# Gathering the tokens of four small experts together, from a normalised copy

## The chip, the cores and the metric

The kernel runs on one core of a Trainium2 chip. The metric is the time of one execution on the device in microseconds (us); three runs of the kernel before took 1511.56 to 1518.7 us, median 1512.85. One further execution was profiled. The engines are TensorE (PE in the profile, its weight loads PEld), VectorE (DVE), ScalarE (ACT), GpSimd (POOL) and SyncE (SP), which here issues every DMA of the weights from its one queue.

## The reference

Two layers of a streaming encoder on 256 tokens of width 1024, all in float32. Layer 0 ends in a dense SwiGLU, layer 1 in a mixture of eight experts of which each token takes two. The change lies in the last part alone:

```python
def moe_swiglu(xn, w_router, w_gate, w_up, w_down):     # xn = rmsnorm(h, norm_ffn_g)
    xt = xn.reshape(-1, d)
    logits = (xt @ w_router).astype(jnp.float32)
    top_vals, top_idx = lax.top_k(logits, TOP_K)
    top_w = jax.nn.softmax(top_vals, axis=-1)
    combine = jnp.sum(one_hot(top_idx, N_EXPERTS) * top_w[..., None], axis=1)
    y = jnp.zeros_like(xt)
    for e in range(N_EXPERTS):
        y = y + combine[:, e:e + 1] * swiglu(xt, w_gate[e], w_up[e], w_down[e])
    return y
# then h = h + y and a final rmsnorm of h
```

Each expert has two weights of 1024 x 3584 and one of 3584 x 1024. All eight are read, 336 loads of 1 MB.

## The kernel before, in words

**Weights.** Class `Stream` reads the weights in chunks of 128 partitions x 2048 floats (`dma`, line 172). `do_split` turns a chunk into two fp32r tiles: `hi` by ScalarE (line 198, a rounded copy) and `lo` by VectorE (line 199, what the rounding left). PE then multiplies with both. All raw chunks, the `hi` and `lo` tiles and a few long-lived ones share one pool of 21 buffers of 8 KB a partition (`R`). When chunk c is split, the load of chunk c+7 is issued (`WIDE_LOAD = 7`); splits run ahead of PE by up to five chunks. A load waits on SP's queue until the buffer that it was given is free, and everything behind it in that queue waits too.

**Places.** After the router, the experts are put in places 0 to 7: place 0 is expert 0, places 1 to 4 are the four experts with the fewest tokens of the others (at most 64 each, "small"), places 5 to 7 the rest (up to 128, "large"). A branch that handles fuller experts is not taken with these inputs. `merged` writes the order by hand: 56 blocks (a block is 512 of an expert's 3584 hidden columns), first three of place 0, then a small and a large one in turn, at the end three of place 4. A block has a gate product, a value product and a down product, each over two chunks; the down product comes two blocks later.

**Gather and scatter.** The tokens of a place are gathered by a product with a one-hot matrix. `Place.gather` makes two such tiles on VectorE: `pg` (line 1134), scaled by the token's 1/rms, and `pb` (line 1138), unscaled. Then PE multiplies 128 x 128 pieces of `h` (from block 3 on of `hs`, a saved copy, line 1303) with `pg` (line 1149): 16 matmuls for a place, of 64 columns for a small and 128 for a large one. ScalarE and VectorE take the result out of PSUM eight pieces at a time (`evict_bank`, lines 278 and 280), since each piece has its own gain column, and leave `xg`. Two transposes of `pb` (line 1157) give the scatter matrix `sc`. When a place's last down product is done, `half` evicts it as `y` (lines 272, 273), and four products `sc` x `y` (`part`, lines 1178 to 1180) add it to `h`.

**Order.** Each engine works in the order in which the code was written, so what is written early waits in front of what follows. Small pieces of PE work are put in a list `later`; `blocks` takes one off at four places of each block (after the gate product, before the down product, before and after the value product). `prepare` of a place makes its one-hot tiles at once, three blocks ahead of the place's first block, and puts its gather products and the transposes in `later`. `done` puts one empty piece and the four `part`s there.

**At the stage's start** the router's sorting steps (lines 1029 to 1059) and the combine weights (1074 to 1079, 1021 to 1024) run on VectorE between the first splits.

Of the kernel before, what the change touches and what calls it, by code (L numbers as in the profile page):

```python
# [21 lines left out]
F32R = mybir.dt.float32r  # L22
# [50 lines left out]

WIDE_LOAD = 7

# [9 lines left out]
def trunk(tc, x, xt_in, mem, mt_in, wa, wb, wc, wl0, wk1, wl1, wff, wmoe, cc, tk, moec, ident_d, gfin, out):  # L85
    nc = tc.nc
    PE, ACT, DVE, POOL = nc.tensor, nc.scalar, nc.vector, nc.gpsimd
    with contextlib.ExitStack() as c:
# [15 lines left out]
        def M(shape, dt=F32, s="m"):  # L104
            return mp.tile(shape, dt, name=nm(s), tag="m")
# [978 lines left out]
        class Final:  # L1084


            def load(self):
                self.x, self.g = R([P, NT, D], s="fin"), R([P, D], s="gf")
                nc.sync.dma_start(out=self.g, in_=gfin)
                self.rms = Rms(h)  # L1090
# [14 lines left out]
            def all(self, part):  # L1105
# [5 lines left out]
                for t in range(NT):  # L1111
                    for n in range(2):
# [3 lines left out]
                        nc.sync.dma_start(out=out[t * P:(t + 1) * P, w], in_=x)  # L1116

        class Place:


            def __init__(self, run, i, small):
                self.run, self.i, self.small = run, i, small
                self.n = HALF if small else P

            def gather(self):

                i, n = self.i, self.n
                slot, r, src = self.run.slot, self.run.r, self.run.src

                def one_hot():  # L1130
                    self.pg = M([P, NT, n], s="pg")
                    self.back_ = M([P, NT, P], s="pb")
                    for t in range(NT):
                        DVE.tensor_scalar(self.pg[:, t, :], iota[:, 0:n], slot[:, t, i:i + 1], r[:, t:t + 1],
                                          op0=OP.is_equal, op1=OP.mult)
                    for t in range(NT):
                        q = P // n
                        DVE.tensor_scalar(self.back_[:, t, :].rearrange("p (q n) -> p q n", q=q),
                                          iota[:, 0:n].unsqueeze(1).to_broadcast([P, q, n]),
                                          slot[:, t, i:i + 1], None, op0=OP.is_equal)  # L1140
                    self.xg = R([P, KC, 2, n], F32R, s="xg")

                def block(k0):
                    m = 512 // n
                    ps = mm()
                    for j in range(m):
                        kk = slice((k0 + j) * P, (k0 + j + 1) * P)
                        for t in range(NT):
                            PE.matmul(ps[:, j * n:(j + 1) * n], src(t)[:, kk], self.pg[:, t, :],  # L1149
                                      start=t == 0, stop=t == NT - 1)  # L1150
                    evict_bank([(self.xg[:, k0 + j, 0], self.xg[:, k0 + j, 1], ps[:, j * n:(j + 1) * n],
                                 col(1, C_FFN + k0 + j)) for j in range(m)])

                def back():
                    ps = mm()
                    for t in range(NT):
                        PE.transpose(ps[:, tok(t)], self.back_[:, t, :], ident)
                    self.scat = M([P, S], F32R, s="sc")
                    ACT.activation(self.scat, ps[:, 0:S], AF.Copy)

                return [one_hot] + [lambda k=k: block(k) for k in range(0, KC, 512 // n)] + [back]
# [21 lines left out]
            def done(self):  # L1183
                later.append(lambda: None)
                for n in range(2):
                    for t in range(NT):
                        later.append(lambda t=t, n=n: self.part(t, n))

        class Block:
# [7 lines left out]
            def product(self, x, out, items, first, last):  # L1197

                if self.small:
                    ops = [(x[0][:, f].rearrange("p i s -> p (i s)"), it[i]) for i in range(2) for f, *it in items]  # L1200
                else:
                    ops = [(x[i][:, f], w) for f, wh, wl in items for i, w in ((0, wh), (0, wl), (1, wh))]
                for i, (a, w) in enumerate(ops):
                    PE.matmul(out, a, w, start=first and i == 0, stop=last and i == len(ops) - 1)  # L1204

            def up(self, out):
                for c in range(2):
                    items = []
                    for i, (wh, wl) in enumerate(self.st.many(2)):
                        items += [(4 * c + 2 * i + q, wh[:, q * 512:(q + 1) * 512], wl[:, q * 512:(q + 1) * 512])  # L1210
                                  for q in range(2)]
                    xg = self.place.xg
                    self.product((xg, None) if self.small else (xg[:, :, 0], xg[:, :, 1]), out, items, c == 0, c == 1)

# [46 lines left out]
            def parts(self):  # L1261
                n = self.place.n
                if self.small:
                    t = M([P, 4, 2, n], F32R, s="hl")
                    self.hl = t, None
                    hi, lo = t[:, :, 0], t[:, :, 1]
                else:
                    hi, lo = self.hl = [M([P, 4, n], F32R, s="hl") for _ in range(2)]
# [21 lines left out]
        class Run:  # L1290
# [4 lines left out]

            def src(self, t):
                return self.saved[0][:, t, :] if self.saved else h[t]
# [71 lines left out]
        def moe(st, routed, weights, sort, combine):  # L1369
# [19 lines left out]
            before = {}  # L1389
            at = {x: i for i, x in enumerate(order)}  # L1390

            def add(i, f):
                before.setdefault(i, []).append(f)
            add(LEAD, run.save)
            for p in range(1, NE):
                add(max(1, at[p, 0] - 3), places[p].prepare)
            run.blocks(st, [(places[p], j) for p, j in order],
                       {i: lambda fs=fs: [f() for f in fs] for i, fs in before.items()})

        def moe_rest(routed):  # L1400
# [8 lines left out]
            st.wide = True  # L1409
            for f in places[0].gather():  # L1410
                f()
            run.blocks(st, [(places[p], j) for p, j in order],
# [137 lines left out]
def _layout(a):  # L1550
# [43 lines left out]
    f["ident"] = np.eye(P, dtype=np.float32)  # L1594
    f["gfin"] = np.ascontiguousarray(np.broadcast_to(a["norm_final_g"][None], (P, D)))
    return f
# [26 lines left out]
```

## Time and profile before

| | |
|---|---|
| median of three runs | 1512.85 us (1511.56 to 1518.7) |
| profiled execution | 1510.55 us, of which span 1508.7 us |
| PE busy | 1469.5 us (97%) |
| DVE busy | 1293.9 us (86%) |
| ACT busy | 1043.2 us (69%) |
| DMA | 459.04 MB, mean 304 GB/s |
| granted TensorE clock | 0.989 of full speed |

The span is the time from the first to the last instruction of the program; 1.85 us of the execution lie around it. The experts' stage begins at about 595 us with the first gather and ends at 1493 us with the last product. Busy PE is not PE at its peak, since matmuls overlap and their ends are modelled; the chain of waits and the distances between matmuls say more. Many matmuls in plain float32 stand in the trace as two records each.

### The profile page before, as it was taken

To read this page: it belongs to the slowest core of one execution; us is meant where nothing else is said; L and a number is where in the kernel's file an instruction comes from. 1 tells how busy PE (TensorE), PEld (TensorE's weight loads), DVE (VectorE), ACT (ScalarE), POOL (GpSimd) and SP (SyncE) were. 2 spreads that over 40 slices of the span, in tenths; PEclk is the share of its full clock that TensorE was granted. 3 is DMA by queue.
4 is the path that set the end of the run, shared out by engine and by line. 5 is a ranking of instruction groups with operands and counts; after the bars stand their busy time and mean duration, and the time that the engine had idled before them with its cause. 6 is when DMAs were issued, how large, how long until landed. Compare 5 with 4: busy or idle time off the path is not lost.

```text
span 1508.7 us, 20807 instructions
## 1 busy us (share of the span) xinstructions
PE 1469.5 (97%) x7757; PEld 1270.9 (84%) x7757; DVE 1293.9 (86%) x1496; ACT 1043.2 (69%) x1224; POOL 7.9 (1%) x23
## 2 busy tenths in 40 slices
PE   8999999999999998999999999999999999999995
PEld 7998988888999897788887878888888888888884
DVE  7988777545698866889999999999999999999996
ACT  7547565434544554688887788887878887888884
POOL 0000000000000001000000000000000000000000
PEclk9999999999999998899999999999999999999998
DMA  9535464544542547399999999999999999999992
GB/s 363 236 112 195 156 247 159 210 178 156 178 178 116 195 168 307 124 376 401 421 381 421 360 403 413 416 386 411 366 397 414 411 392 386 390 403 415 421 421 86
DMA packets 65326, 459.04 MB, mean 304 GB/s; under 512 B 7232, under 2 KB 7744, under 8 KB 11840
## 3 DMA queue, kind: packets, MB, share of 16 engines
q1 hardware_dynamic: 65216, 457.62, 76.5%
q8 instruction: 63, 1.03, 0.3%
q14 instruction: 47, 0.39, 0.1%
HBM read 456.55 MB, written 1.05 MB: 303 GB/s over the span
## 4 chain that ended last, share of the span: by engine, by line
PE 90%; DVE 4%; issue 2%; ACT 2%; DMA 1%; POOL 0%; SPq 0%; DVEq 0%; ACTq 0%; POOLq 0%
PE mm L1204 31%; PE acc L1204 16%; PE mm L220 5%; PE mm L222 5%; PE mm L221 5%; PE mm L1227 3%; PE acc L221 3%; PE acc L222 3%; PE acc L220 3%; PE mm L463 3%; PE z L221 2%; PE z L222 2%; PE z L220 2%; DVE lo L199 2%; PE mm L1149 2%
## 5 line engine op out<-in xcount | busy, mean ns | idle before, releaser
L199 DVE TENSOR_TENSOR lo<-w,hi 128x2048 fp32r<-128x2048 f32 (+3 forms) x504 | 946.4, 1917 | 56.9 <-ACT hi L198 37.8
L198 ACT ACTIVATE hi<-w 128x2048 fp32r<-128x2048 f32 (+3 forms) x504 | 795.1, 1619 | 111.9 <-PE mm L1204 58.0
L1204 PE MATMUL mm<-hi,xg 128*128 128x512 f32 x1344 | 405.4, 393 | 1.6 <-ACT xg L278 1.2
L1204 PEld LDWEIGHTS mm<-hi,xg 128*128 128x128 f32 x1344 | 253.0, 189 | 53.7 <-ACT xg L278 1.4
L1204 PE MATMUL mm<-lo,xg 128*128 128x512 f32 x896 | 295.3, 391 | 0.0
L1204 PE MATMUL acc<-hi,hl 128*128 128x512 f32 x672 | 217.4, 398 | 0.0
L1204 PEld LDWEIGHTS mm<-lo,xg 128*128 128x128 f32 x896 | 168.8, 188 | 34.1
L1204 PE MATMUL acc<-lo,hl 128*128 128x512 f32 x448 | 157.7, 393 | 0.0
L1204 PEld LDWEIGHTS acc<-hi,hl 128*128 128x128 f32 x672 | 125.2, 189 | 24.4
L1204 PEld LDWEIGHTS acc<-lo,hl 128*128 128x128 f32 x448 | 84.8, 189 | 17.4
L220 PE MATMUL z<-hi,xt 128*128 128x320 f32 (+1 forms) x256 | 79.0, 308 | 7.0 <-ACT xt L338 7.0
L221 PE MATMUL z<-lo,xt 128*128 128x320 f32 (+1 forms) x256 | 77.9, 304 | 0.2 <-DVE lo L199 0.2
L222 PE MATMUL z<-hi,xt 128*128 128x320 f32 (+1 forms) x256 | 78.0, 304 | 0.0
L548 DVE SCALAR_TENSOR_TENSOR ca<-ca,cct 128x256 f32<-128x256 f32 x180 | 77.1, 482 | 0.2
L220 PE MATMUL mm<-hi,xt 128*128 128x512 f32 (+1 forms) x192 | 71.9, 375 | 0.0
L222 PE MATMUL mm<-hi,xt 128*128 128x512 f32 (+1 forms) x192 | 71.5, 372 | 0.0
L221 PE MATMUL mm<-lo,xt 128*128 128x512 f32 (+1 forms) x192 | 71.4, 372 | 0.0
L1227 PEld LDWEIGHTS mm<-twice,gu 128*128 128x128 f32 x448 | 58.3, 191 | 6.0 <-ACT gu L1217 2.1
L1227 PE MATMUL mm<-twice,gu 128*128 128x64 f32 x448 | 56.2, 268 | 2.0 <-ACT gu L1217 2.0
L220 PEld LDWEIGHTS z<-hi,xt 128*128 128x128 f32 x256 | 49.7, 194 | 7.2 <-ACT xt L338 7.0
L221 PEld LDWEIGHTS z<-lo,xt 128*128 128x128 f32 x256 | 49.6, 194 | 0.5 <-DVE lo L199 0.5
L222 PEld LDWEIGHTS z<-hi,xt 128*128 128x128 f32 x256 | 49.5, 193 | 0.0
(284 smaller groups left out, 1891.5 us busy)
## 6 DMA issues: line engine op xcount, KB each, us to landing
w<-in_wmoe_dram SPq DMA_DIRECT2D x336, 1024.0 KB, 8.0
w<-in_wl_dram SPq DMA_DIRECT2D x39, 1024.0 KB, 4.8
w<-in_wff_dram SPq DMA_DIRECT2D x33, 1024.0 KB, 4.8
w<-in_wb_dram SPq DMA_DIRECT2D x8, 960.0 KB, 8.9
w<-in_wa_dram SPq DMA_DIRECT2D x5, 1024.0 KB, 4.9
w<-in_wc_dram SPq DMA_DIRECT2D x8, 640.0 KB, 4.6
tk<-in_tk_dram SPq DMA_DIRECT2D x2, 1024.0 KB, 10.5
mt<-in_mem_t_dram SPq DMA_DIRECT2D x2, 1024.0 KB, 8.2
```

The source lines that it names most:

```text
L198: ACT.activation(hi[:, ws], r, AF.Copy)
L199: DVE.tensor_tensor(lo[:, ws], r, hi[:, ws].bitcast(F32), op=OP.subtract)
L220: PE.matmul(ps, ah, bh, start=start, stop=False)
L221: PE.matmul(ps, ah, bl, start=False, stop=False)
L222: PE.matmul(ps, al, bh, start=False, stop=stop)
L463: PE.matmul(self.kps[:, d, :], w[:, ks], self.mt[:, k, :], start=k == 0, stop=k == KC - 1)
L548: return lambda: DVE.scalar_tensor_tensor(dst, src[:, k:k + S], w, dst, op0=OP.mult, op1=OP.add)
L1149: PE.matmul(ps[:, j * n:(j + 1) * n], src(t)[:, kk], self.pg[:, t, :], start=t == 0, stop=t == NT - 1)
L1204: PE.matmul(out, a, w, start=first and i == 0, stop=last and i == len(ops) - 1)
L1227: PE.matmul(ps[:, f * n:(f + 1) * n], w, twice, start=True, stop=True)
```

## The change

The saved copy of the tokens is now normalised: `save` writes `hn` = h x 1/rms (ScalarE, two instructions) x gain (VectorE, two instructions; the gain comes by a new DMA of 512 KB, `gn`). It is made at block 1 instead of block 3. All four small places are gathered from it by one set of products with a 256-column one-hot `pgs` (`gather_small`): four pieces of PE work, each four matmuls and one eviction by ACT and one by DVE of 128 x 512. Large places 5 to 7 are gathered from `hn` with `pb` itself, so their `pg` is gone, and they too are evicted 512 columns at a time. Place 0 is gathered as before, but its `pb` is made after the sorting. A small place's `pb` and `sc` are made at its last block. `prepare` puts an empty piece in front, `done` two instead of one. `WIDE_LOAD` is 6 instead of 7.

```diff
-WIDE_LOAD = 7
+WIDE_LOAD = 6
...
-            def gather(self):
-                i, n = self.i, self.n
-                slot, r, src = self.run.slot, self.run.r, self.run.src
+            def gather_raw(self):
+                pg = M([P, NT, P], s="pg")
                 def one_hot():
-                    self.pg = M([P, NT, n], s="pg")
-                    self.back_ = M([P, NT, P], s="pb")
...
+                    self.hot(pg, self.run.r)
+                    self.xg = R([P, KC, 2, P], F32R, s="xg")
...
+                return [one_hot, lambda: block(0), lambda: block(4), self.spread, self.back]
+            def gather(self):
+                self.xg = R([P, KC, 2, P], F32R, s="xg")
+                def block(k0):
                     ps = mm()
+                    for j in range(4):
+                        kk = slice((k0 + j) * P, (k0 + j + 1) * P)
+                        for t in range(NT):
+                            PE.matmul(ps[:, j * P:(j + 1) * P], self.run.saved[0][:, t, kk], self.pb[:, t, :],
+                                      start=t == 0, stop=t == NT - 1)
+                    evict_hl(self.xg[:, k0:k0 + 4, 0], self.xg[:, k0:k0 + 4, 1],
+                             ps.rearrange("p (k s) -> p k s", k=4))
+                return [lambda: block(0), lambda: block(4)]
             def prepare(self):
-                first, *rest = self.gather()
-                first()
-                later.extend(rest)
+                self.spread()
+                later.append(lambda: None)
+                if not self.small:
+                    later.extend(self.gather())
+                later.append(self.back)
...
             def done(self):
-                later.append(lambda: None)
+                later.extend([lambda: None] * 2)
...
+            def load(self):
+                self.g = R([P, D], s="gn")
+                nc.sync.dma_start(out=self.g, in_=gfin[1])
             def save(self):
-                self.saved.append(R([P, NT, D], s="hs"))
-                for t in range(NT):
-                    ACT.activation(self.saved[0][:, t, :], h[t], AF.Copy)
+                hn = R([P, NT, D], s="hn")
+                self.saved.append(hn)
+                for t in range(NT):
+                    ACT.activation(hn[:, t, :], h[t], AF.Copy, scale=self.r[:, t:t + 1])
+                for t in range(NT):
+                    DVE.tensor_tensor(hn[:, t, :], hn[:, t, :], self.g, op=OP.mult)
+            def gather_small(self, places):
+                pg = M([P, NT, SMALL * HALF], s="pgs")
+                for q, p in enumerate(places):
+                    p.hot(pg[:, :, q * HALF:(q + 1) * HALF])
+                xs = [R([P, 4, SMALL, 2, HALF], F32R, s="xs") for _ in range(2)]
...
+                def block(k0):
+                    ps = mm()
+                    for j in range(2):
+                        kk = slice((k0 + j) * P, (k0 + j + 1) * P)
+                        for t in range(NT):
+                            PE.matmul(ps[:, j * 256:(j + 1) * 256], self.saved[0][:, t, kk], pg[:, t, :],
+                                      start=t == 0, stop=t == NT - 1)
+                    to = xs[k0 // 4][:, k0 % 4:k0 % 4 + 2]
+                    evict_hl(to[:, :, :, 0], to[:, :, :, 1], ps.rearrange("p (k q s) -> p k q s", k=2, q=SMALL))
+                return [lambda k=k: block(k) for k in range(0, KC, 2)]
...
-            first = places[0].gather()
-            later.append(first.pop())
-            later.append(combine)
-            for i, f in enumerate(first):
+            first = places[0].gather_raw()
+            for i, f in enumerate(first[:3]):
                 f()
                 if i == 0:
                     for _ in range(PRESPLIT):
                         st.do_split()
                     weights()
+                    run.load()
             sort()
+            first[3]()
+            later.extend([first[4], combine])
...
-            add(LEAD, run.save)
+            def start_small():
+                run.save()
+                later.append(lambda: None)
+                later.extend(run.gather_small(places[1:1 + SMALL]))
+            add(1, start_small)
             for p in range(1, NE):
-                add(max(1, at[p, 0] - 3), places[p].prepare)
+                add(max(2, at[p, 0] - 3) if p > SMALL else at[p, NJ - 1], places[p].prepare)
```

`hot` and `spread` write the one-hot tiles `pg`/`pgs` (line 1152 of the new kernel) and `pb` (line 1161). In the new kernel lines 1234, 1256, 1258 are the old 1204, 1227, 1229, and lines 1208 to 1210 the old 1178 to 1180.

First place, VectorE at block 1 of place 0, before: `lo` are splits, `a` is the gated product of block 0, `pg` and `pb` belong to place 1, the first small one, `xg` is its gathered input, `hl` the split of block 0's hidden values.

```order
L199 TENSOR_TENSOR lo_5845<-w_5694,hi_5844 128x2048
L199 TENSOR_TENSOR lo_5861<-w_5696,hi_5860 128x2048
L1247 TENSOR_TENSOR a_5825<-mm_5843,a_5825 128x512
L1134 TENSOR_SCALAR pg_5877<-mct,slotp,t_5611 128x64 x2
L1138 TENSOR_SCALAR pb_5878<-mct,slotp 128x128 x2
L199 TENSOR_TENSOR lo_5886<-w_5698,hi_5885 128x2048
L199 TENSOR_TENSOR lo_5914<-w_5700,hi_5913 128x2048
L280 SCALAR_TENSOR_TENSOR xg_5883<-mm_5933,cct,xg_5883 128x64 x8
L1271 TENSOR_TENSOR hl_5972<-mm_5966,hl_5971 128x512
```

The same place now:

```order
L199 TENSOR_TENSOR lo_5847<-w_5691,hi_5846 128x2048
L199 TENSOR_TENSOR lo_5863<-w_5693,hi_5862 128x2048
L1276 TENSOR_TENSOR a_5827<-mm_5845,a_5827 128x512
L1337 TENSOR_TENSOR hn_5879<-hn_5879,gn_5721 128x1024 x2
L1152 TENSOR_SCALAR pgs_5884<-mct,slotp 128x64 x8
L199 TENSOR_TENSOR lo_5897<-w_5695,hi_5896 128x2048
L199 TENSOR_TENSOR lo_5913<-w_5697,hi_5912 128x2048
L1301 TENSOR_TENSOR hl_5948<-mm_5942,hl_5947 128x512
L273 TENSOR_TENSOR xs_5893<-mm_5951,xs_5893 128x8x64
```

Where two one-hots of 64 columns and two of 128 stood between `a` and the next splits, two products of 128 x 1024 and eight one-hots of 64 columns stand now.

Second place, TensorE in the middle of the stage, before: the end of a large block's gate product, the gather of place 2 (`pg`, `hs`), then the transposes of a small block (`gu`) and a small block's down product (`acc`).

```order
L1204 MATMUL mm_7485<-lo_7423,xg_6845 128x512
L1204 MATMUL mm_7485<-hi_7422,xg_6845 128x512
L1149 MATMUL mm_7524<-pg_7478,hs_6142 128x64 x16
L1227 MATMUL mm_7557<-twice,gu_7469 128x64 x4
L1157 MATMUL mm_7563<-ident,pb_7479 128x128 x2
L1204 MATMUL acc_7568<-hi_7441,hl_7418 128x512
```

The same place now:

```order
L1234 MATMUL mm_7459<-lo_7400,xg_6838 128x512
L1234 MATMUL mm_7459<-hi_7399,xg_6838 128x512
L1256 MATMUL mm_7498<-twice,gu_7446 128x64 x4
L1234 MATMUL acc_7504<-hi_7418,hl_7395 128x512
```

The gather and the two transposes of place 2 are gone from here; the gather is in the four pieces at the start, the transposes are at place 2's last block.

Third place, TensorE where the output of place 1 is first read, before: `y` is the evicted down product, and it is read right behind a value product.

```order
L1204 MATMUL mm_7958<-hi_7900,xg_7484 128x512 x4
L1204 MATMUL mm_7958<-lo_7901,xg_7484 128x512 x4
L1178 MATMUL mm_7989<-y_7949,sc_5978 128x512
L1179 MATMUL mm_7989<-y_7949,sc_5978 128x512
L1227 MATMUL mm_7993<-twice,gu_7914 128x64 x4
L1204 MATMUL mm_8000<-hi_7921,xg_6845 128x512
```

The same place now (24 matmuls of the next gate product are cut to their first and last):

```order
L1234 MATMUL mm_7902<-lo_7845,xs_5894 128x512 x4
L1256 MATMUL mm_7933<-twice,gu_7858 128x64 x4
L1234 MATMUL mm_7940<-hi_7865,xg_6838 128x512
...
L1234 MATMUL mm_7940<-hi_7883,xg_6838 128x512
L1208 MATMUL mm_7979<-y_7893,sc_7625 128x512
L1209 MATMUL mm_7979<-y_7893,sc_7625 128x512
```

The first reading of `y` has moved behind the transposes and a whole gate product.

## Rows read from the trace of the kernel before

**Rows 1.** The page: busy times, and GB/s in 40 equal slices of the span.

```profile
PE 1469.5 (97%) x7757; PEld 1270.9 (84%) x7757; DVE 1293.9 (86%) x1496; ACT 1043.2 (69%) x1224; POOL 7.9 (1%) x23
...
GB/s 363 236 112 195 156 247 159 210 178 156 178 178 116 195 168 307 124 376 401 421 381 421 360 403 413 416 386 411 366 397 414 411 392 386 390 403 415 421 421 86
```

**Rows 2.** Stretches: us, busy PE, PEld, DVE, ACT, POOL, PEclk, DMA share, GB/s.

```profile
829.70:1051.10 221.40, 218.52 (x1065) 183.33 (x1065) 212.62 (x149) 180.49 (x148) 0.00 (x0) 1.00 0.99 399
1200.00:1300.00 100.00, 98.35 (x484) 82.43 (x482) 95.90 (x70) 81.66 (x69) 0.00 (x0) 1.00 0.95 381
```

**Rows 3.** Who waited for whom, 640 to 1508: us, times, longest.

```profile
ACT hi L198 <- PE mm L1204: 58.0, 57, 3.0
...
PE mm L1179 <- DVE y L273: 4.5, 5, 1.2
PE mm L1149 <- DVE pg L1134: 4.4, 3, 1.5
```

**Rows 4.** Waits of SP's own queue, 640 to 1508.

```profile
SPq L172 <- PE mm L1204: 360.3, 154, 5.1
SPq L172 <- PE acc L1204: 227.9, 84, 7.1
SPq L172 <- DVE lo L199: 63.1, 35, 5.9
```

**Rows 5.** Tile w (raw chunks), 640 to 1508: duration ns min/median/max.

```profile
L199 DVE TENSOR_TENSOR lo<-w,hi x324: 2280/2290/2307, 639.4 to 1484.9; 128x2048 fp32r<-128x2048 f32 x162
...
L172 SPq DMA_DIRECT2D w<-in_wmoe_dram x315: 327/333/788, 647.1 to 1465.0; - x158
...
DMA to landing us min/median/max: 4.7/8.1/14.2
```

**Rows 6.** Chain of waits before place 3's gather: start, us, what.

```profile
1049.54 1.17 issue
1050.71 0.33 DVE pg L1134
...
1051.08 3.79 PE mm L1149 x32
```

**Rows 7.** Chain of waits at the output of place 2.

```profile
1108.47 0.70 DVE y L273
...
1109.21 0.50 PE mm L1179
```

**Rows 8.** Groups by form: busy us, mean ns, idle before.

```profile
L1149 PE MATMUL mm<-pg,hs 128*128 128x128 f32 x96 | 11.7, 275 | 0.0
L1149 PE MATMUL mm<-pg,hs 128*128 128x64 f32 x96 | 11.4, 277 | 4.4 <-DVE pg L1134 4.4
...
L280 DVE SCALAR_TENSOR_TENSOR xg<-mm,cct,xg 128x128 fp32r<-128x128 f32 x32 | 8.6, 345 | 3.1 <-ACT xg L278 3.1
...
L280 DVE SCALAR_TENSOR_TENSOR xg<-mm,cct,xg 128x64 fp32r<-128x64 f32 x32 | 6.5, 276 | 5.2 <-ACT xg L278 5.2
```

**Rows 9.** Groups by form before 590: a float32 product of 256 columns.

```profile
L463 PE MATMUL mm<-mt,w 128*128 128x256 f32 x176 | 39.1, 381 | 0.0
```

**Rows 10.** Order of time at the stage's start: start us, us, instruction.

```profile
622.58 0.69 DVE L1247 TENSOR_TENSOR a<-mm,a 128x512 f32<-128x512 f32 x1
623.18 0.53 DVE L1134 TENSOR_SCALAR pg<-mct,slotp,t 128x64 f32<-128x64 f32 x2
623.63 0.48 DVE L1138 TENSOR_SCALAR pb<-mct,slotp 128x128 f32<-128x128 f32 x2
623.64 6.38 PE L1149 MATMUL mm<-pg,h 128*128 128x64 f32 x32 [3.14 <-DVE pg L1134]
...
630.94 0.78 PE L1204 MATMUL mm<-hi,xg 128*128 128x512 f32 x1
```

**Rows 11.** Stretches of TensorE: us, busy, PEclk, DMA share, GB/s.

```profile
623.00:624.00 1.00, 0.36 (x4) 1.00 0.52 74
624.00:634.60 10.60, 10.60 (x46) 0.52 0.23 94
634.60:640.00 5.40, 5.40 (x25) 1.00 0.61 206
```

More of the change, by code (lines that the diff above doesn't have):

```diff
@@ L1088, in load @@
                 self.x, self.g = R([P, NT, D], s="fin"), R([P, D], s="gf")
-                nc.sync.dma_start(out=self.g, in_=gfin)
+                nc.sync.dma_start(out=self.g, in_=gfin[0])
                 self.rms = Rms(h)
@@ L1116, in all, with part @@
                         nc.sync.dma_start(out=out[t * P:(t + 1) * P, w], in_=x)
+        def part(x, i):
+            return x[i] if type(x) is tuple else x[:, i]
         class Place:
@@ L1154, in back @@
-                def back():
-                    ps = mm()
[L1156 to L1161, printed above, removed]
-            def prepare(self):
-                first, *rest = self.gather()
-                first()
-                later.extend(rest)
+                    evict_bank([(self.xg[:, k0 + j, 0], self.xg[:, k0 + j, 1], ps[:, j * P:(j + 1) * P],
+                                 col(1, C_FFN + k0 + j)) for j in range(4)])
@@ new lines, in gather_raw, with hot @@
+                return [one_hot, lambda: block(0), lambda: block(4), self.spread, self.back]
+            def hot(self, out, r=None):
+                for t in range(NT):
+                    c = self.run.slot[:, t, self.i:self.i + 1]
+                    if r is None:
+                        DVE.tensor_scalar(out[:, t, :], iota[:, 0:self.n], c, None, op0=OP.is_equal)
+                    else:
+                        DVE.tensor_scalar(out[:, t, :], iota[:, 0:self.n], c, r[:, t:t + 1], op0=OP.is_equal, op1=OP.mult)
@@ new lines, in spread, with back @@
+            def spread(self):
+                self.pb = M([P, NT, P], s="pb")
+                for t in range(NT):
+                    q = P // self.n
+                    DVE.tensor_scalar(self.pb[:, t, :].rearrange("p (q n) -> p q n", q=q),
+                                      iota[:, 0:self.n].unsqueeze(1).to_broadcast([P, q, self.n]),
+                                      self.run.slot[:, t, self.i:self.i + 1], None, op0=OP.is_equal)
+            def back(self):
+                ps = mm()
+                for t in range(NT):
+                    PE.transpose(ps[:, tok(t)], self.pb[:, t, :], ident)
+                self.scat = M([P, S], F32R, s="sc")
+                ACT.activation(self.scat, ps[:, 0:S], AF.Copy)
@@ new lines, in gather @@
+            def gather(self):
+                self.xg = R([P, KC, 2, P], F32R, s="xg")
+                def block(k0):
+                    ps = mm()
+                    for j in range(4):
+                        kk = slice((k0 + j) * P, (k0 + j + 1) * P)
[5 more added lines that the diff above has]
+                return [lambda: block(0), lambda: block(4)]
@@ L1199, in product @@
                 if self.small:
-                    ops = [(x[0][:, f].rearrange("p i s -> p (i s)"), it[i]) for i in range(2) for f, *it in items]
+                    ops = [(x(f).rearrange("p i s -> p (i s)"), it[i]) for i in range(2) for f, *it in items]
                 else:
-                    ops = [(x[i][:, f], w) for f, wh, wl in items for i, w in ((0, wh), (0, wl), (1, wh))]
+                    ops = [(part(x(f), i), w) for f, wh, wl in items for i, w in ((0, wh), (0, wl), (1, wh))]
                 for i, (a, w) in enumerate(ops):
@@ L1211, in up @@
                                   for q in range(2)]
-                    xg = self.place.xg
-                    self.product((xg, None) if self.small else (xg[:, :, 0], xg[:, :, 1]), out, items, c == 0, c == 1)
+                    self.product(self.place.x(), out, items, c == 0, c == 1)
             def copy(self, ps):
@@ L1264, in parts @@
                     t = M([P, 4, 2, n], F32R, s="hl")
-                    self.hl = t, None
+                    self.hl = lambda f: t[:, f]
                     hi, lo = t[:, :, 0], t[:, :, 1]
                 else:
-                    hi, lo = self.hl = [M([P, 4, n], F32R, s="hl") for _ in range(2)]
+                    hi, lo = t = [M([P, 4, n], F32R, s="hl") for _ in range(2)]
+                    self.hl = lambda f: (t[0][:, f], t[1][:, f])
                 v = self.a.rearrange("p (f s) -> p f s", f=4)
@@ L1409, in moe_rest @@
             st.wide = True
-            for f in places[0].gather():
-                f()
+            places[0].prepare()
+            while later:
+                pe_later()
             run.blocks(st, [(places[p], j) for p, j in order],
@@ L1594, in _layout @@
     f["ident"] = np.eye(P, dtype=np.float32)
-    f["gfin"] = np.ascontiguousarray(np.broadcast_to(a["norm_final_g"][None], (P, D)))
+    f["gfin"] = np.stack([np.broadcast_to(g[None], (P, D)) for g in (a["norm_final_g"], a["norm_ffn_g"][1])])
     return f
```

23 lines of the change are left out of this document (8 added, 15 removed).

## The prediction

> **What bounds the kernel now.** I read the page's busy line first: PE is busy for 97% of the span [rows 1]. That alone proves little, so next come the stretches of the experts' stage. One period of the stage (a small and a large expert, 84 loads of 1 MB, 221.4 us, so 2.64 us a load) has PE at 218.52, DVE at 212.62 and the DMA engines at a share of 0.99 with 399 GB/s [rows 2]. The reader is to see three resources within 4% of each other. Which of them is waited for? The list of waits answers: ACT's splits wait for PE to free a buffer (58.0 us), and SP's queue waits for PE to free one too (360.3 and 227.9 us, against 63.1 for DVE) [rows 3, 4]; PE is never kept waiting by a split or a load there. So PE is the bound, and it loses time only where a small instruction of DVE comes late: 4.4 us for one-hot tiles in three waits, 4.5 us for `y` in five [rows 3]. The chain shows both: DVE comes out of its splits, makes `pg`, and PE starts [rows 6]; DVE makes the lower half of `y`, and PE starts [rows 7]. Last I read the order of time at the stage's start, where PE idles for 3.14 us and then runs for some 10 us at half clock [rows 10, 11].
>
> **The change, part by part.**
>
> *Gather of the small places.* Before, each takes 32 records of 64 columns. They cost 11.4 us for 96, 0.119 each, and the records of 128 columns cost the same (11.7 us for 96) [rows 8]: below 128 columns the number of records sets the price. A whole place takes 3.79 us on PE with nothing beside it [rows 6]. Places 2 to 4 lose theirs: 3 x 3.79 = -11.4 us. In their stead the common gather has 16 matmuls, again 32 records, of 256 columns. The nearest row for those is 39.1 us for 176, 0.222 each [rows 9]: 7.1 us for all four places, 1.8 us a piece. It stands at the start and is counted there. Bounds for a record: 0.119 (as at 64 columns) to 0.476 (four times that, if columns alone counted), 3.8 to 15.2 us in all; I take the row of the same width and type.
>
> The Trainium skill (TensorE: Matmul & The Clock Gate, Back-to-back issue gap) gives about 109 ns for a warm matmul of 256 columns. By that, as an estimate, the 32 records would take 3.5 us and the sum would come 3.6 us lower; this case's float32 row shows twice the page's figure, and I go by the row.
>
> *Waits for one-hots.* The three late `pg` tiles are those of places 2 to 4 (the first waits are gone with their gather): -4.4 us [rows 3]. A large place now needs only `pb`, made a piece earlier than it is read; a piece is at least 16 matmuls of a weight product, several us, and the lateness was at most 1.5 us [rows 3].
>
> *Output read a piece later.* What was late by up to 1.2 us now has the next gate product ahead of it: -4.2 us of the 4.5, since the last place's output stands at the end with nothing behind to cover it. Next late there would be the splits, which kept ahead of PE throughout.
>
> *DVE and ACT in the middle.* A period's DVE loses eight small evictions (6.5/32 x 8 = 1.6 us), turns eight larger ones (2.15 us, at 8.6/32) into two of 512 columns (about 1.4, estimated at 0.7 each from `a`, [rows 8, 10]), and loses `pg` twice (about 1.1): some -3.5 us, to 209. The new period is 221.4 - 3.8 - 1.5 - 1.2 = 214.9 us, so DVE would be 97% busy, as PE before. I cost this at nothing: PE covers it, at a margin of 6 us a period.
>
> *The start.* This is where the change costs. Before, DVE finishes `a` at 623.27 and `pg`, and PE gathers from 623.64, at half clock, until the value product starts at 630.94 [rows 10]. Now place 0's `pb` stands ahead of three splits (+0.48), and behind `a` come two products of 128 x 1024, about 1.15 each (half a split of 2.29, [rows 5]), and eight one-hots at 0.27: 2.3 + 2.1. PE's first piece then starts at 623.27 + 0.48 + 4.4 = 628.2, after an idle time of some 7 us broken only by four transposes. With one piece of 1.8 us (3.6 at half clock) the value product starts at 630.0 to 631.8, about as before. But three more pieces follow before the first small block, 3 x 1.8 = 5.3 us. So the start costs +5.3; the half-clock stretch, 10.6 us at 0.52 [rows 11], could be over sooner (+4) or last as long after the later restart and cost another 2.3 to 4 (+8 to +10).
>
> Here the Trainium skill speaks against the change: the same page (Why this matters for your kernels) warns of idle gaps between bursts of matmuls because the clock falls back to half. The trace agrees in kind (0.52 behind the 3.14 us gap); a gap of twice that length is shown by no row, which is why the upper end of the start stands at +10.
>
> *Loads.* `WIDE_LOAD` 6 issues each load one chunk later. Before, seven loads ahead are 7 x 2.64 = 18.5 us, less 651/315 = 2.1 us of queue wait a load [rows 4, 5] and 8.1 us to landing: some 8 us in hand. Now 6 x 2.56 - 2.1 - 8.1 = 5 us in hand at the median, and none for the slowest (14.2 us). In the middle PE's own distance behind the splits covers the rare late one. At the end, where only small blocks are left and PE asks faster than the slices' 421 GB/s [rows 1] deliver, less is in hand: +1 us (bounds 0 and one load, 2.6). The new DMA of 512 KB goes out before the sorting is done, in a gap of the queue: nothing.
>
> Sum against the profiled execution of 1510.55 us: -11.4 - 4.4 - 4.2 + 5.3 + 1.0 = -13.7, so 1496.9. The median of the runs shown lies 2.3 us above that execution: 1499.
>
> **Rivals.**
>
> *DVE takes the wait over.* At 97% DVE is so full that its next late instruction (a small block's `a`, a split) stops PE instead. For it: all waits of PE now are for DVE. Against it: no split was ever late in 840 us, and DVE loses work. If half of the 20 us saved in the middle comes back as new waits: 1499 + 7 = 1506 with a little of the rest kept.
>
> *The start costs double.* Two long gaps with half clock over all four pieces and a value product: +10 instead of +5.3, 1504. For it: the gap doubles. Against it: the clock came back in the trace while PE was at work.
>
> *The loads become the bound: slower.* With one buffer fewer in the queue, loads come late steadily, PE stands still, frees buffers later, and the next loads start later still. It decides once queue wait and landing together pass 15.4 us at the median instead of 10.2. Price: the pace of the slowest 100 us, 381 GB/s [rows 2], is 2.75 us a load, 0.11 over today's; over some 300 loads +33 us, half of that if it holds half the time; what is saved on PE is then lost in waiting for loads: 1513 + 2 to 1513 + 33, 1515 to 1545. For it: a DMA share of 0.99. Against it: SP waits for buffers, not for the engines behind it.
>
> *Columns set the price,* so the common gather is no cheaper: 15.2 us instead of 7.1, of which three quarters fall into the start: 1507. Against it: the 256-column row.
>
> **How the numbers follow.** The forecast has a chance of 0.62, with its own range of 1493 to 1504; DVE 0.15; the start 0.10; the loads 0.08; the columns 0.05. A measurement of this kernel tells about 0.5%, 7.6 us, from no change. Faster by more than that (under 1505.3) is all of the forecast, most of the start and a third of DVE: 0.76. Slower by more (over 1520) is most of the loads' case: 0.07. Between lies 0.17. The range that should hold 8 in 10 is 1491 to 1511: it leaves out the loads' case and some of a better outcome (a cheap record and a short half-clock stretch, about 1491).
>
> **What would show it.** No matmul of a gather between 660 us and the large places' own; 32 records of 256 columns at about 0.22; no PE wait for `y` or a one-hot in the middle, periods of about 215 us; PE idle for some 7 us near 621 to 628 us, and the first small block 5 us later than before; SP still waiting mostly for PE. Wrong would be: ACT waiting for DMA in the middle (loads), PE waiting for `lo` or `a` (DVE), periods still near 221 us.

## The result and the profile after

The changed kernel takes 1497.1 us (four runs, 1495.95 to 1497.54) against 1512.78 us for the kernel before: a ratio of 0.9884, 95% interval 0.9859 to 0.9909. The forecast was 1499. The span of the profiled execution went from 1508.7 to 1495.4 us. So the sum came out; the experiments will show that one of its terms had the wrong sign, and that two others had more than the cause that was named.

Two periods of the stage, after (the columns of [rows 2]):

```profile
829.70:1045.70 216.00, 214.74 (x1034) 179.91 (x1033) 208.87 (x131) 177.03 (x135) 0.00 (x0) 1.00 1.00 410
1045.70:1261.70 216.00, 214.74 (x1035) 179.84 (x1034) 208.87 (x131) 177.00 (x134) 0.00 (x0) 1.00 1.00 408
```

A period has become 5.4 us shorter (221.4 in [rows 2]), 2.57 us a load. PE's busy time fell by 3.78, one gather of 3.79 [rows 6], and its idle time from 2.88 to 1.26. DVE lost 3.75 us and is 97% busy.

Waits of the kernel after, 640 to 1495 us (the columns of [rows 3]):

```profile
ACT hi L198 <- PE mm L1234: 53.1, 54, 3.4
DVE lo L199 <- ACT hi L198: 17.5, 22, 1.8
PEld mm L1258 <- DVE a L1276: 7.1, 9, 1.1
...
PE mm L1258 <- DVE a L1276: 3.8, 6, 0.6
...
PE mm L1256 <- ACT gu L1246: 2.9, 1, 2.9
ACT hi L198 <- DMA w<-in_wmoe_dram: 1.1, 3, 0.5
...
PE mm L1209 <- DVE y L273: 0.2, 1, 0.2
```

The 4.4 us for `pg` are gone and of the 4.5 us for `y` [rows 3] 0.2 remain, at the very end. New are six waits for `a` (a large block's gated product, which PE transposes next), twice a period; by the distance between matmuls, which counts somewhat more than the idle time of these lists, each costs PE 0.79 us. Before there were three of 0.34 us; these are their line and that of the wait for `gu` (the copy of a small block's product) at the end, in the trace of the kernel before:

```profile
PE mm L1227 <- ACT gu L1217: 2.0, 1, 2.0
...
PE mm L1229 <- DVE a L1247: 0.5, 3, 0.2
```

The six new waits stand at the end of a chain that the order of time shows whole (start, us, instruction, idle time before and what ended it):

```profile
809.98 5.52 ACT L198 ACTIVATE hi<-w 128x2048 fp32r<-128x2048 f32 x3 [2.26 <-PE mm L1234]
811.93 2.29 DVE L199 TENSOR_TENSOR lo<-w,hi 128x2048 fp32r<-128x2048 f32 x1 [1.82 <-ACT hi L198]
...
814.14 0.68 DVE L1276 TENSOR_TENSOR a<-mm,a 128x512 f32<-128x512 f32 x1
...
814.88 0.66 PE L1258 MATMUL mm<-ident,a 128*128 128x128 f32 x4 [0.63 <-DVE a L1276]
```

ACT does not split the next chunk before PE frees a buffer for `hi`; DVE makes `lo` behind it; `a` was written behind that `lo` and waits its turn, though the product that it reads had ended at 810.2 us; PE waits for `a`. DVE is late here because it was held up, not because it is full: it had been idle for 1.82 us. The same pair of rows stands in the trace before, ahead of place 3's late `pg` [rows 6]:

```profile
1029.51 5.52 ACT L198 ACTIVATE hi<-w 128x2048 fp32r<-128x2048 f32 x3 [2.26 <-PE mm L1204]
1031.46 2.29 DVE L199 TENSOR_TENSOR lo<-w,hi 128x2048 fp32r<-128x2048 f32 x1 [1.83 <-ACT hi L198]
```

From there DVE worked on without a gap until `pg` at 1050.71: the delay was carried for 19 us to where it was paid. The prediction read the first line of [rows 3] as a sign that PE is the bound; it is the head of this chain too.

The start, after (the columns of [rows 10]):

```profile
622.04 0.69 DVE L1276 TENSOR_TENSOR a<-mm,a 128x512 f32<-128x512 f32 x1
622.64 2.35 DVE L1337 TENSOR_TENSOR hn<-hn,gn 128x1024 f32<-128x1024 f32 x2
622.78 0.42 PEld L1258 LDWEIGHTS mm<-ident,a 128*128 128x128 f32 x4 [2.65 <-DVE a L1276]
...
624.91 1.39 DVE L1152 TENSOR_SCALAR pgs<-mct,slotp 128x64 f32<-128x64 f32 x8
626.19 2.99 PEld L1353 LDWEIGHTS mm<-pgs,hn 128*128 128x128 f32 x8 [2.99 <-DVE pgs L1152]
```

and two stretches of TensorE (the columns of [rows 2]):

```profile
625.65:629.06 3.41, 2.87 (x7) 2.34 (x8) 3.41 (x6) 0.00 (x0) 0.00 (x0) 0.50 0.77 283
629.10:634.60 5.50, 5.50 (x26) 4.58 (x25) 5.34 (x5) 4.21 (x3) 0.00 (x0) 1.00 0.48 183
```

The stretch at half clock (granted 0.50, the lower of the two levels) is 3.4 us long, against 10.2 before (10.6 us at a mean of 0.52 in [rows 11]), though PE idles longer ahead of it: 2.23 and 2.75 us with the transposes between them, against 3.14. The value product is done 3.35 us earlier than before; three later pieces of 1.71 us (records 0.213 us apart) then bring the first small block to 656.9 us, 1.8 us later than before.

### The profile page after: what moved, and what is told of

The parts are those of the page before. It is cut to its first block, busy times and chain, and to the rows that moved or that the text cites. A ratio compares the mean times of both kernels' runs of the same rounds, so it can differ in the third digit from the quotient of the medians.

```text
span 1495.4 us, 20502 instructions
## 1 busy us (share of the span) xinstructions
PE 1456.5 (97%) x7661; PEld 1258.0 (84%) x7661; DVE 1286.7 (86%) x1446; ACT 1034.6 (69%) x1178; POOL 7.8 (1%) x23
## 4 chain that ended last, share of the span: by engine, by line
PE 93%; DVE 3%; DMA 1%; ACT 1%; issue 1%; POOL 0%; SPq 0%; DVEq 0%; POOLq 0%; ACTq 0%
PE mm L1234 32%; PE acc L1234 17%; PE mm L220 5%; PE mm L222 5%; PE mm L221 5%; PE acc L221 3%; PE acc L222 3%; PE acc L220 3%; PE mm L1256 3%; PE mm L463 3%; PE z L221 2%; PE z L222 2%; PE z L220 2%; PE mm L492 2%; PE mm L1258 1%
## 5 line engine op out<-in xcount | busy, mean ns | idle before, releaser
L1234 PE MATMUL mm<-hi,xg 128*128 128x512 f32 x896 | 288.0, 393 | 2.2 <-ACT xg L278 1.7
L1234 PEld LDWEIGHTS mm<-hi,xg 128*128 128x128 f32 x896 | 168.4, 188 | 36.7 <-ACT xg L278 1.9
L1234 PE MATMUL mm<-lo,xg 128*128 128x512 f32 x448 | 174.7, 390 | 0.0
L1234 PE MATMUL mm<-hi,xs 128*128 128x512 f32 x448 | 120.3, 390 | 0.0
L1234 PE MATMUL mm<-lo,xs 128*128 128x512 f32 x448 | 119.9, 390 | 0.0
L1234 PEld LDWEIGHTS mm<-lo,xs 128*128 128x128 f32 x448 | 84.1, 188 | 17.4
L1234 PEld LDWEIGHTS mm<-lo,xg 128*128 128x128 f32 x448 | 84.2, 188 | 16.5
L1234 PEld LDWEIGHTS mm<-hi,xs 128*128 128x128 f32 x448 | 83.8, 188 | 17.1
```

## The experiments

Each ratio is to the kernel before, run beside the variant; its interval reaches some 0.25% (3.8 us) to either side in most of them. So the large steps (14 us and more) are shown by the times, while differences of 2 to 4 us between variants are not: there the traces decide, by the stretch from the first small block to the first use of the sixteenth chunk from the end ("the middle": 796.1 us in the kernel before, 779.7 in the changed one).

**A seventh load in flight again.**

```diff
-WIDE_LOAD = 6
+WIDE_LOAD = 7
```

> The changed kernel with seven loads in flight again instead of six. Theory (the sixth-load prefetch costs only at the end): the middle keeps its period of 216.0 us, PE's wait of 2.9 us for gu near 1465 us shrinks by about half, so about 1.5 us faster than the changed kernel, 1495.6 us. Rival 1 (six loads keep the loads late everywhere, 2.9 us between landing and split instead of 5.5): periods fall too, 3 us or more faster. Rival 2 (the buffer that the seventh load takes is missed by the split tiles): ACT waits longer for PE, the six waits of PE for a of 0.79 us grow, 2 to 4 us slower, 1499 to 1501 us.

Measured: 1520.84 us (ten runs), ratio 1.0033 (1.0021 to 1.0045) against 0.9884 for the changed kernel: by the ratios 23 us slower. Without this constant all the rest of the change is a small loss. Its waits, 640 to 1495 us:

```profile
ACT hi L198 <- PE mm L1234: 119.4, 57, 5.0
DVE lo L199 <- ACT hi L198: 44.3, 30, 2.3
...
PE mm L1258 <- DVE a L1276: 21.8, 25, 1.1
```

Rival 2 has the mechanism and was far too small: ACT's wait for buffers doubles, and PE waits for `a` once in every pair of a small and a large block, mostly 1.24 us, 25.7 us in all. The middle is 21.7 us longer than in the changed kernel, nearly all of it these waits. The period is 221.4 us again, with no gather of a small place in it:

```profile
829.00:1050.40 221.40, 215.57 (x1034) 179.33 (x1033) 208.89 (x131) 176.75 (x135) 0.00 (x0) 1.00 0.98 399
```

**The kernel before with six loads.**

```diff
-WIDE_LOAD = 7
+WIDE_LOAD = 6
```

> The kernel before with six loads in flight instead of seven and nothing else changed. Theory (only the end notices): 1 to 2 us slower than the kernel before, 1513.8 to 1514.8 us, with the loss after 1450 us. Rival (the loads become the bound): periods of the middle grow from 221.4 us by 4 to 9 us, 15 us or more slower. Rival 2 (nothing hangs on the seventh load): within 0.5 us.

Measured: 1500.77 us, ratio 0.9905 (0.9879 to 0.9931). None of the three: by the ratios the constant alone gives 0.95 of the 1.16%, with every gather still in its place. Its period and its waits, 640 to 1495 us:

```profile
829.00:1047.60 218.60, 218.20 (x1066) 183.26 (x1066) 212.59 (x149) 181.53 (x148) 0.00 (x0) 1.00 0.99 405
```

```profile
ACT hi L198 <- PE mm L1204: 47.2, 65, 1.3
...
PE mm L1179 <- DVE y L273: 1.4, 4, 0.4
PEld mm L1149 <- DVE pg L1134: 1.2, 3, 0.4
```

DVE's work in a period is the same as before (212.59 against 212.62 [rows 2]), and PE's idle time falls from 2.88 to 0.40 us. So a full DVE was not what made `pg` and `y` late. The longest wait of a split fell from 3.0 to 1.3 us, and PE's waits for `pg` went with it. The middle is 8.2 us shorter than in the kernel before; the waits for `pg`, `y` and `a` account for 8.0 (4.5, 2.5 and 1.0).

This also says what the rest of the change is worth on top of six loads: 0.21% by the ratios, with intervals that overlap, so the times alone do not show it. In the traces the middle of the changed kernel is 8.2 us shorter than here (three gathers gone, six waits for `a` come in), but its first small block starts 2.7 us later and its end takes 3.5 us more.

**Six loads, but one buffer fewer.** Is it the load, or the buffer it takes?

```diff
-R_BUFS = 21
+R_BUFS = 20
```

> The changed kernel, six loads in flight as in it, but the pool that raw loads, split tiles and long-lived tiles share has 20 buffers instead of 21. Theory (a seventh load costs because it takes a buffer from the split tiles; the waits of PE for a, pg and y are the end of a chain PE frees a buffer, ACT splits, DVE splits, DVE's small instruction): the splits are left with as few buffers as with seven loads, so waits of about 1.2 us for a at every second small block come back, 1515 to 1521 us. Rival (what costs is the seventh load itself, by when it is issued or by its traffic): no change, within 2 us of 1497.1 us.

Measured: 1521.34 us, ratio 1.0054 (1.0035 to 1.0073). Its waits, 640 to 1495 us:

```profile
ACT hi L198 <- PE mm L1234: 119.5, 57, 5.0
DVE lo L199 <- ACT hi L198: 44.4, 30, 2.3
...
PE mm L1258 <- DVE a L1276: 21.8, 25, 1.1
```

These are the waits of the seven-load kernel, line for line to 0.1 us, and ACT waits for no load in either. The theory holds for the changed kernel: what counts is how many of the shared buffers are left for the split tiles. The mirror of it, seven loads and one buffer more, was not run. The Trainium skill (Perfetto Trace Analysis, Optimization Strategy) says that one and the same gap coming again on the engine that should be full can mean too few buffers for the next tile; the trace agrees, with a gap of 1.24 us (0.37 at a few places) that returns every 30 to 35 us.

**Five loads in flight.**

```diff
-WIDE_LOAD = 6
+WIDE_LOAD = 5
```

> The changed kernel with five loads in flight. Theory (one more buffer for the splits): the six waits of 0.79 us for a go, -4.7 us, against up to 2 us more at the end, where the last loads are late: 1493 to 1496 us. Rival (the loads become the bound, since a load is now 2.6 us later and only 2.9 us lay between landing and split): ACT waits for DMA throughout, periods above 216 us, 1502 us or more.

Measured: 1495.28 us, in the theory's range, but the ratio 0.9882 (0.9858 to 0.9906) is that of the changed kernel: the times show no gain. The trace shows the theory's two parts, a middle 5.2 us shorter and an end that loses 2.0 us more; a start that was 1.7 us later takes some of the rest. A period and the waits that matter:

```profile
829.00:1043.30 214.30, 214.30 (x1034) 180.10 (x1033) 209.39 (x131) 179.91 (x135) 0.00 (x0) 1.00 1.00 412
```

```profile
ACT hi L198 <- PE mm L1234: 39.4, 55, 1.3
ACT hi L198 <- DMA w<-in_wmoe_dram: 33.1, 65, 1.0
...
PE mm L1256 <- ACT gu L1246: 4.9, 1, 4.9
```

PE is not idle at all in the period, although DVE is 98% busy. Now loads come late at 65 splits, but the distance that the splits keep ahead of PE covers that until the end, where `gu` stands behind splits that wait for loads, and PE loses 4.9 us instead of 2.9.

**The kernel before with five loads.** The same constant in the kernel before, `WIDE_LOAD = 5`.

> The kernel before with five loads in flight. Theory (the split tiles were the ones short of buffers; six already removed the waits for pg and a, five frees one more buffer than PE needs): the three waits for y of 0.56 us that were left with six go, 0 to 2 us faster than with six, 1498.5 to 1501 us. Rival (the loads become the bound): slower than with six by 3 us or more.

Measured: 1500.2 us, ratio 0.9899 (0.9871 to 0.9928): no different from six within the intervals. The three waits for `y` stayed, at 0.47 us; that part of the theory missed.

**Each small place gathered by itself.** The common gather alone undone:

```diff
+            def gather_one(self):
+                pg = M([P, NT, HALF], s="pgs")
+                self.hot(pg)
+                self.xg = R([P, KC, 2, HALF], F32R, s="xs")
...
-                later.extend(run.gather_small(places[1:1 + SMALL]))
             add(1, start_small)
+            for p in range(1, 1 + SMALL):
+                add(max(1, at[p, 0] - 3), places[p].gather_one)
```

> The changed kernel, but each small place is gathered by itself again, from the normalised copy: 16 matmuls (32 records) of 64 columns and one eviction pair, places 2 to 4 three blocks ahead of their first block, place 1 at the start; the common gather alone is undone. Theory (the number of records sets the price, 0.107 us each at full clock): +3 x 3.4 = 10.2 us in the middle, at the start 3.4 us instead of 4 x 1.7 = 6.8 us and 1.0 us less of one-hots: 10.2 - 3.4 - 1.0 = 5.8 us slower, 1502.9 us. Rival (columns set the price, 64 columns cost a quarter of 256): 4 x 0.85 instead of 6.8 us, 3.4 to 4.4 us faster, 1493 us. Rival 2 (what PE saves in the middle comes back as waits for DVE): the private gathers only fill such waits, within 1 us of the changed kernel, and the 0.79 us waits for a go.

Measured: 1500.84 us, ratio 0.9899 (0.9873 to 0.9925); the spans of the two profiled executions are 1498.9 and 1495.4. About two thirds of the theory's 5.8 us, with intervals that overlap. Its period shows what the times do not:

```profile
829.00:1047.00 218.00, 218.00 (x1069) 183.73 (x1067) 210.54 (x134) 179.31 (x136) 0.00 (x0) 1.00 0.99 405
```

PE works 3.3 us more a period, as the theory has it (32 records of 64 columns, 0.112 us apart), and in the middle the 0.79 us waits for `a` are all gone, which it did not have: +10.2 became +5.6 there. At the start it had 4.4 us to gain and gained 0.7, with 10.2 us at half clock. A record of 64 columns costs half of one of 256 (0.213), not a quarter, so the gather term stands. That the common gather costs the splits a buffer, as it holds two tiles where this one mostly holds one, fits this; it was not tried by itself.

**The output read a piece earlier again.**

```diff
-                later.extend([lambda: None] * 2)
+                later.append(lambda: None)
```

> The changed kernel with one empty piece instead of two in front of the reading of a place's output. Theory (the later reading removes the waits for y): three waits for y of about 1.4 us come back, and three of the waits for a fall from 0.79 to 0.34 us: +4.2 - 1.4 = 2.8 us slower, 1499.9 us. Rival (DVE sets the pace, so a wait that is removed in one place returns in another): within 0.5 us of 1497.1 us.

Measured: 1499.98 us, ratio 0.9896 (0.987 to 0.9923), 2.9 us above the changed kernel between the medians, with intervals that overlap; the middle is 2.1 us longer. In its trace, 640 to 1495 us:

```profile
PE mm L1209 <- DVE y L273: 4.5, 5, 1.2
...
PE mm L1258 <- DVE a L1276: 1.5, 6, 0.3
```

The waits for `y` are back at the 4.5 us of [rows 3], and the waits for `a` are shorter for it (three of 0.33 and three of 0.46 us instead of six of 0.79). Here DVE's delay is paid at whichever of the two PE reads first.

**The common gather one block later.**

```diff
-                later.append(lambda: None)
                 later.extend(run.gather_small(places[1:1 + SMALL]))
-            add(1, start_small)
+            add(2, start_small)
```

> The changed kernel with the normalised copy and the common gather begun at block 2 instead of block 1, without the empty piece. Theory (at block 1 PE idles 2.75 us for the one-hots because DVE is behind there; one block later DVE is ahead): this idle time and some of the half-clock stretch go, the first small block starts 3 to 4 us earlier, 1493 to 1494 us. Rival (the 3.7 us of DVE work delay the splits of block 2, or the small places' input is late for block 3): nothing gained, 1497 us, or slower.

Measured: 1493.97 us (1492.19 to 1497.52), ratio 0.9868 (0.9843 to 0.9893). In its profiled execution the idle time for the one-hots is 0.32 us:

```profile
637.81 1.97 PE L1353 MATMUL mm<-pgs,hn 128*128 128x256 f32 x8 [0.32 <-DVE pgs L1152]
```

but `a` of block 0 comes 1.5 us later in this execution, before anything that was edited (623.57 against 622.04), so that the first small block starts only 0.9 us earlier, and the last load lands at 1466.3 us as in the changed kernel (1466.1). The median is lower by the size that was expected, but the intervals overlap, and the profiled execution, the slowest of the four, gains nothing on the changed kernel's (span 1495.7 against 1495.4 us). That the shorter idle time is worth 3 us is not shown.

**Two small pieces ahead of the transposes of `a`.**

```diff
                     b.gate()
-                    pe_later()
+                    pe_later(2)
```

> The changed kernel with two pieces of small PE work instead of one taken between a block's gate product and the transposes of a. Theory (a is late by a fixed time there, set by the buffer that PE freed before): a product of y and sc of 0.45 us more covers part of it, six waits fall from 0.79 to 0.34 us, 2.7 us faster, 1494.4 us. Rival (the wait moves with PE's work, or y is read too early again): within 0.5 us, or waits for y.

Measured: 1496.99 us, ratio 0.9895 (0.987 to 0.992): nothing. All six waits for `a` fell, three to 0.33 and three to 0.15 us, 3.3 us in all. But at three other places the second piece is the transposes of a `pb` that DVE makes right behind `a`, and PE waits 0.66 us (0.5 as idle time) for that:

```profile
PE mm L1168 <- DVE pb L1161: 1.5, 3, 0.5
...
PE mm L1258 <- DVE a L1276: 0.5, 3, 0.2
```

The middle is 1.1 us shorter, which the times do not resolve.

**The small blocks of the end spread out.**

```diff
-            for i in range(max(len(large) - LEAD, len(small))):
-                order += small[i:i + 1] + large[LEAD + i:LEAD + i + 1]
+            large, small = large[LEAD:], small[:]
+            while large or small:
+                n = 2 if len(large) in (16, 8) else 1
+                order += small[:n] + large[:1]
+                large, small = large[1:], small[n:]
```

> The changed kernel with another order of the blocks: two of the three small blocks that stand together at the end are moved to about a third and two thirds of the stage, where a load in hand can cover them. Theory (at the end PE works through small blocks at 2.0 us a load and the loads come at about 2.5, so PE waits 3.1 us for gu there and the clock falls): the wait near 1465 us goes or falls under 1 us, 2 to 4 us faster, 1493 to 1495 us. Rival (the end is bound by the loads as a whole, the last one lands at 1466 us whatever the order): the last load lands at the same time, under 1 us gained, or slower since more of a block's work stands behind the last load.

Measured: 1499.33 us, ratio 0.9892 (0.9864 to 0.9921): no gain, as the rival had it. The last load lands at 1464.8 us, 1.3 us earlier, the wait for `gu` falls only to 2.2 us, more work stands behind the last load, and one wait for `a` grows to 1.24 us.

**Five loads and the later gather; and both with the spread order.** The edits above together.

> The changed kernel with five loads in flight and the common gather begun at block 2. Theory (the two gains lie in different places and the end takes back what the loads can't follow): no wait for a in the middle, the first small block at about 656 us, PE waits 5 us or more for gu near the end; last load at 1464 to 1465 us as with five loads alone, 1493 to 1495 us. Rival (they add up in full, 3.5 + 3 us): 1490 us.

> Five loads in flight, the common gather at block 2 and the spread order of blocks together. Theory (buffers for the splits in the middle, loads at the end): the middle without waits for a, the wait at the end under 2 us: 1488 to 1492 us. Rival (the loads bind everywhere with five in flight): 1495 us or more, ACT waiting for DMA in the middle.

Measured: 1491.83 us, ratio 0.9851 (0.9824 to 0.9877), the lowest median that was run, between the theory's range and the rival: the middle has no wait for `a`, but the first small block comes at 654.1 us instead of 656 and the last load at 1460.4. With the spread order 1493.92 us, ratio 0.9862 (0.9839 to 0.9884), outside its theory's range: PE's wait for `gu` at the end is 4.7 us where less than 2 was expected, and one long wait for `a` stays. In the first, PE waits at the end:

```profile
1460.47 1.91 ACT L198 ACTIVATE hi<-w 128x2048 fp32r<-128x2048 f32 x1 [0.49 <-DMA w<-in_wmoe_dram]
1462.28 0.58 ACT L1246 ACTIVATE gu<-mm 128x512 f32<-128x512 f32 x1
...
1462.91 1.97 PE L1256 MATMUL mm<-twice,gu 128*128 128x64 f32 x8 [5.04 <-ACT gu L1246]
```

## Why the prediction was right, and where it was not

Up to the first use of the sixteenth chunk from the end (1451.1 us before, 1436.5 after) the ledger, in the distances between PE's matmuls, is: start +1.8, three gathers -11.4, `pg` 3 x 1.63 = -4.9, `y` 3 x 1.38 = -4.1, new waits for `a` 6 x 0.79 - 3 x 0.34 = +3.7; sum -14.9 against the -14.6 measured.

- **Gather: right.** -11.4, with 0.213 us for a record of 256 columns where 0.222 was taken. The row of this kernel was the better guide: the figure of the Trainium skill (TensorE: Matmul & The Clock Gate, Back-to-back issue gap), about 109 ns, is half of what the trace shows for these float32 records. By that figure the sum would have come 2.7 us lower, not 3.6 as the prediction has it, since only three of the four pieces stand in the sum.
- **One-hots and output: right in size, not in reason.** The `pg` waits also go (to 0.13 us each) when nothing but the number of loads changes. They were the bill of a split that came late for want of a buffer. For `y`, six loads alone leave 0.56 us of 1.38, and in the changed kernel the later reading does what was said: undone, it brings three waits of 1.38 us back, and the middle is 2.1 us longer.
- **"Next late there would be the splits": wrong.** Next late was `a`, +3.7 us. The rival "DVE takes the wait over" named the symptom, but for a full DVE; with 98% and five loads there was no wait.
- **Loads: the step that failed.** "`WIDE_LOAD` 6 issues each load one chunk later ... +1 us." It weighed only what a shorter queue could cost, and gave no worth to the buffer that comes free. Measured, the constant is worth 8.2 us of the middle and 0.95% (14 us) in all in the kernel before, and 21.7 us of the middle and some 23 us in all in the changed one. The sum came out because two things that it left out nearly cancel. The waits that six loads remove were booked under one-hots and output; and the rest of the change seems to take a buffer from the splits: with seven loads it has 25.7 us of waits for `a`, which go to 4.7 when the constant gives a buffer back. That cancelling is luck: had the change kept seven loads, the same steps would have forecast some 1498 us; measured are 1520.84.
- **The start: too dear by 3.5 us.** The three pieces behind the value product cost 5.1 us as forecast. But the value product began at 629.2 us, 1.7 ahead of the kernel before, where it was to begin about as before (the eight one-hots took 1.39 us, not 2.1, and the stage's first weight product had begun 0.9 us earlier, at 602.0); and its two chunks took 5.4 us instead of 7.1, as the clock came back after 3.4 us of half speed instead of 10.2. The 0.9 us and the shorter half-clock stretch are luck: over all the runs the first product began between 601.3 and 603.6 us, and the same start with the output read earlier had 6.8 us at half clock.
- **The end: right in kind.** From that chunk to the last one's first use PE took 40.2 us before and 42.0 after, +1.8 against +1.0: the wait for `gu` rose from 2.0 to 2.9 us, and 6.8 us at half clock follow it, against 3.4 before:

```profile
1468.74:1475.57 6.83, 6.83 (x21) 5.67 (x22) 5.05 (x5) 0.51 (x2) 0.00 (x0) 0.50 0.00 0
```

Two rivals are priced otherwise than their own terms give: half of 20 us that comes back as waits would be +10 and not +7 (1509 us), and three quarters of the 8.1 us of dear columns would be +6.1 (1505). The forecast uses neither.

What stays open: which of the long-lived tiles takes the buffer that makes the changed kernel so much more sensitive (23 us against 14; that it is one of them is argued, not shown), and what sets the end, where the last load lands at 1459 to 1471 us in the changed kernel and its variants other than the two that leave the splits a buffer less.

## What to carry to other kernels

When loads, split tiles and long-lived tiles share one pool, the depth of prefetch is paid in buffers of the stage behind it: count the buffers left for each, and vary the depth and the pool by one before crediting a gain to anything else. A small instruction that comes late need not be on a full engine: look back along its engine for the last idle time, and at what ended that. A forecast can hit the time with a term of the wrong sign: here undoing one part at a time showed it, and the total did not.

## What was not expected of the hardware

The stretch at half clock (granted 0.50) at the start lasted 10.2 us in the kernel before and 6.8 us in the same kernel with six loads (625.9 to 632.7), each after the same 3.14 us of idle PE; 3.4 us in the changed kernel and 6.8 us in the variant with the earlier output, whose start is the same code. With the later gather it lasted 3.4 us, with five loads besides there was none, and with the spread order besides, which leaves the start as it is, 3.4 us again, each time after a first wait of 2.2 us. At the end a wait of 2.5 us left the clock full (six loads, kernel before), while waits of 2.0 (kernel before), 2.2 (spread order) and 2.9 us (changed kernel) were followed by 3.4, 6.8 and 6.8 us at half. So in these traces the length of the wait does not say how long the clock stays low. In both pairs with the same start the difference is 3.4 us at half clock, an estimated 1.7 us of PE's work (half of it), and a forecast of a few us there can't be closer than that.
